# The stick-breaking scan takes the score tile in PSUM as its second operand, and the planner costs a scan at two cycles an element

## The chip, the cores and the metric

The kernel runs on one core of one Trainium2 chip. The metric is device time in microseconds (us), the median of several runs. The engines are named as in the profile: PE (TensorE matmuls), PEld (its weight loads), DVE (VectorE), ACT (ScalarE), POOL (GpSimd) and SP (the queue that issues the transfers). SBUF is the on-chip memory that all of them use, PSUM the small memory into which PE writes.

## The reference

A decoder trunk of two layers over one sequence of 1024 tokens, width 1024. Each layer is a mixing sub-layer (a stick-breaking attention branch and a latent-attention branch, fed by one input projection, gated and merged) and a squared-ReLU MLP of width 4096. The change touches only the weights of the stick-breaking branch: 8 heads of width 64, query blocks of 128 rows, each against all keys up to its own block.

```
z = q @ k.T * scale                                    # one block: 128 x end
log_fail = where(mask, log_sigmoid(-z), 0)
later    = reverse_cumsum(log_fail, keys) - log_fail
w        = where(mask, exp(log_sigmoid(z) + later), 0)
o        = w @ v
```

In products instead of logs: with F = sigmoid(-z) and W = sigmoid(z), the weight of key s is W[s] times the product of F over all later keys. Masked scores are so low that their F is 1 and their W is 0.

## The kernel before

**Recording and planning.** The program first records every operation (`record`) with its engine, its tiles and a duration from a table of costs (`cost`). A planner (`schedule`) then runs a list schedule with these durations: each of PE, ACT, DVE, POOL and the transfers picks, whenever it is free, the ready operation with the earliest due time. Due times are counted back from the order in which PE's operations were recorded. At last `emit` issues all operations by planned start time, and each engine works through its own queue strictly in that order. The semaphores between engines are put in by the framework beneath, from the order in which the operations are issued and the tiles that they touch. All helper calls go through line 213, so the profile's rows all read L213 and are told apart by tiles.

**One unit.** In the stick-breaking stage a layer works through 4 pairs of heads, 2 heads of a pair, 8 query blocks of a head: 64 units a layer, 128 in all. Block j has n = 128 (j + 1) keys. A unit is:

1. PE: scores into `sc`, a tile of 128 x 1024 in PSUM. There are two such tiles (`sc0`, `sc1`).
2. ACT: `F` = sigmoid(-z) and `W` = sigmoid(z), both read from `sc` and written to SBUF.
3. DVE: the scan, in place over `F`, from the last key to the first: a running product. Its second operation is `bypass`, so the second operand's values do not enter the result; before, that operand is `F` itself.
4. POOL: `W` times the scanned `F`, shifted by one key.
5. Two units later PE transposes `W` in groups of four blocks into `tp`, a PSUM tile of which there are two. ACT copies the group rounded to `wth`, DVE puts the rest into `wtl`; then the `tp` tile is free.
6. After every second unit PE multiplies `wth` and `wtl` with the values, into a `tp` tile again. ACT and DVE take the result out as `O`.

Between the units PE does "fill": the input projections of later pairs and gates (`pp<-H,parts`), whose weights are split by ACT and POOL (`parts`). In layer 0 the sums for the conditioning vector (`AD`, `A`) run on DVE as well. Then follows the latent-attention stage, the output projections and the MLP.

**The cost of a scan.** For DVE `cost` gives 0.069 us plus one cycle (1/960 us) an element, a scan included.

Of the kernel before, what the change touches and what calls it, by code (L numbers as in the profile page):

```python
# [15 lines left out]
ALU = mybir.AluOpType  # L16
# [159 lines left out]
class Plan:  # L176
# [13 lines left out]
    def record(self, engine, method, a, k):  # L190
# [14 lines left out]
        op.early = self.early  # L205
        op.func = str(k.get("func", "")).split(".")[-1]
        op.dur = cost(op.eng, method, a, k, outs, ins)
        op.succs, op.news, op.tiles = [], [], []
        nc = self.nc
# [216 lines left out]
def width(v):  # L426
    n = 1
    if v.dims is not None:
        for a, b in [(x, y) for _, x, y in v.dims[1:]]:
            n *= b - a  # L430
        return n
    for a, b in v.box[1:]:
        n *= b - a
    return n


def cost(eng, method, a, k, outs, ins):

    if eng == "DMA":
        v = (outs + ins)[0]  # L440
        n = 1
        for x, y in v.box:
            n *= y - x
        return n * 4 / 360e3
    n = width(outs[0])
    if eng == "PE":
        dt = str(ins[0].tile.dtype)
        if "32r" in dt:
            return 0.107 if n < 16 else (n if n >= 256 else 4 * n) / 2400.0 + 0.003
        if "bfloat" in dt:  # L450
            return n / 2400.0 + 0.003
        return 0.109 if method == "transpose" else 0.13
    psum = any(getattr(v.tile.cls, "psum", False) for v in ins)
    if eng == "ACT":
        x = 0.052 if psum else 0.093
        if isinstance(k.get("bias"), View):
            x += 0.093
        if k.get("accum_out") is not None:
            x += 0.093
        return x + n / 1200.0  # L460
    if eng == "DVE":
        if method == "reduce_max":
            n = width(ins[0])
        x = 0.069 + n / 960.0
        if method == "scalar_tensor_tensor" and len(ins) > 2:
            x += 0.06
        if method in ("tensor_scalar", "tensor_copy") and not psum:
            x = 0.069 + n / 1920.0 + (0.06 if len(ins) > 1 else 0)
        return x
    if method == "memset":  # L470
        return 0.036 + n / 1200.0
    if method == "tensor_scalar":
        return 0.26 + n * 3.33e-3
    return 0.15 + n * 2.1e-3
# [12 lines left out]
class Trunk:  # L487
# [553 lines left out]
    def sb_weights(self, ps, j):  # L1041
        nc = self.nc
        n = (j + 1) * P
        F, W = self.full(self.c_F), self.full(self.c_W)
        nc.scalar.activation(out=F[:, :n], in_=ps[:, :n], func=AF.Sigmoid, scale=-0.125)
        nc.scalar.activation(out=W[:, :n], in_=ps[:, :n], func=AF.Sigmoid, scale=0.125)
        rev = F[:, :n][:, ::-1]
        nc.vector.tensor_tensor_scan(out=rev, data0=rev, data1=rev, initial=1.0, op0=ALU.mult, op1=ALU.bypass)
        nc.gpsimd.tensor_mul(W[:, : n - 1], W[:, : n - 1], F[:, 1:n])
        return W  # L1050

# [658 lines left out]
```

## Time and profile before

| | us |
|---|---|
| Median of 3 runs | 3334.44 (3331.59 to 3336.16) |
| The profiled execution | 3345.88, its span 3344.1 |
| PE busy over the span | 3116.7 (93%) |
| DVE busy | 2295.3 (69%) |
| ACT busy | 1544.1 (46%) |
| POOL busy | 1243.2 (37%) |
| The 128 scans on DVE | 235.4 |

The two stick-breaking stages lie at about 294 to 606 us (layer 0) and 1990 to 2277 us (layer 1) of the span. A row of the timeline gives start, duration, engine, operation, output<-input, shape and, in brackets, how long the engine had stood idle and whose work ended that. In the rows by group the numbers behind the bar are busy time, mean duration in ns, and idle time of the engine just before.

### The profile page before, as it was taken

What the parts mean: (1) busy time and instruction counts of PE and PEld (TensorE: products, weight loads), DVE (VectorE), ACT (ScalarE), POOL (GpSimd) and SP (SyncE); (2) the same over time, 40 slices, a digit from 0 to 9 for tenths busy, and PEclk for the clock granted to TensorE, in tenths of its full rate; (3) what the DMA queues carried; (4) which work ended last, traced back from release to release, by engine and by line L of the source; (5) the groups of instructions that cost most, each with busy time, mean ns of one, the idle gap of its engine ahead of it and who ended that gap; (6) DMA issues with size and microseconds to landing.
All of it is one profiled execution on the core that took longest, in us unless ns stands there. A gap on an engine that the chain in (4) does not pass through costs nothing.

```text
span 3344.1 us, 42801 instructions
## 1 busy us (share of the span) xinstructions
PE 3116.7 (93%) x14823; PEld 2519.9 (75%) x14823; DVE 2295.3 (69%) x3238; ACT 1544.1 (46%) x2643; POOL 1243.2 (37%) x952
## 2 busy tenths in 40 slices
PE   5999899999998989998999998999999989999998
PEld 4877677778776777776777877778887767888886
DVE  7443677768567687799986326766675777658786
ACT  4443455657344434433344335556664444444434
POOL 3222344211234654344533223442112456544542
PEclk8999999999999999999999999999999999999999
DMA  6456455545844555876333474344457436467522
GB/s 216 148 164 187 119 150 141 143 129 155 273 128 126 187 189 174 258 237 206 104 103 91 131 219 130 105 126 108 112 167 243 133 104 204 155 199 255 181 76 89
DMA packets 450268, 532.46 MB, mean 159 GB/s; under 512 B 32498, under 2 KB 320900, under 8 KB 450052
## 3 DMA queue, kind: packets, MB, share of 16 engines
q1 hardware_dynamic: 450052, 529.72, 51.8%
q8 instruction: 118, 1.93, 0.3%
q14 instruction: 98, 0.80, 0.1%
HBM read 367.60 MB, written 162.00 MB: 158 GB/s over the span
## 4 chain that ended last, share of the span: by engine, by line
PE 61%; DVE 18%; DMA 11%; issue 4%; ACT 3%; POOL 1%; SPq 1%; DVEq 0%; ACTq 0%; POOLq 0%
PE pp L213 50%; PE tp L213 7%; PE sc L213 4%; DVE A L213 4%; DVE T L213 3%; DVE F L213 3%; DMA AD<-in_w_ada 3%; DMA T<-dram 2%; DVE x L213 2%; DMA dram<-T 1%; DVE wtl L213 1%; DVE bo L213 1%; DVE u L213 1%; POOL parts L213 1%; DMA vT<-dram 1%
## 5 line engine op out<-in xcount | busy, mean ns | idle before, releaser
L213 PE MATMUL pp<-H,parts 128*128 128x512 f32 x4032 | 1060.4, 407 | 13.5 <-ACT H L213 11.4
L213 PEld LDWEIGHTS pp<-H,parts 128*128 128x128 f32 x4032 | 742.3, 191 | 165.4 <-ACT H L213 13.1
L213 PE MATMUL pp<-bo,ws 128*128 128x512 f32 x2688 | 642.4, 400 | 28.0 <-POOL ws L213 15.7
L213 POOL TENSOR_TENSOR parts<-raw,parts 128x1024 fp32r<-128x1024 f32 (+2 forms) x168 | 370.1, 2204 | 758.0 <-ACT parts L213 699.2
L213 PEld LDWEIGHTS pp<-bo,ws 128*128 128x128 f32 x2688 | 506.7, 190 | 151.0 <-POOL ws L213 18.8
L213 POOL TENSOR_TENSOR ws<-wr,ws 128x1024 fp32r<-128x1024 f32 x112 | 295.7, 2647 | 367.2 <-ACT ws L213 335.3
L213 PE MATMUL pp<-t,pw 128*128 128x512 f32 x1344 | 322.0, 397 | 9.8 <-ACT u L213 9.5
L213 PEld LDWEIGHTS pp<-t,pw 128*128 128x128 f32 x1344 | 251.0, 189 | 70.4 <-ACT u L213 10.5
L213 DVE TENSOR_TENSOR_SCAN F<-F 128x128 f32<-128x128 f32 (+7 forms) x128 | 235.4, 1848 | 90.3 <-ACT F L213 90.2
L213 ACT CAST parts<-raw 128x1024 fp32r<-128x1024 f32 (+2 forms) x168 | 151.9, 904 | 265.1 <-PE pp L213 228.0
L213 PE MATMUL pp<-b,pw 128*128 128x512 f32 x1008 | 248.6, 404 | 14.4 <-DVE u L213 14.4
L213 ACT CAST wth<-tp 128x512 fp32r<-128x512 f32 (+3 forms) x384 | 180.8, 481 | 153.1 <-PE tp L213 147.9
L213 DVE TENSOR_TENSOR wtl<-tp,wth 128x512 fp32r<-128x512 f32 (+3 forms) x384 | 205.5, 548 | 64.8 <-ACT wth L213 62.9
L213 POOL TENSOR_TENSOR W<-W,F 128x127 f32<-128x127 f32 (+7 forms) x128 | 168.6, 1321 | 210.4 <-DVE F L213 117.5
L213 DVE SCALAR_TENSOR_TENSOR x<-pp,const,x 128x512 f32<-128x512 f32 x256 | 181.7, 740 | 90.6 <-PE pp L213 90.6
L213 POOL TENSOR_TENSOR pw<-T,pw 128x512 fp32r<-128x512 f32 x112 | 165.0, 1489 | 208.5 <-ACT pw L213 208.0
L213 PEld LDWEIGHTS pp<-b,pw 128*128 128x128 f32 x1008 | 191.3, 192 | 62.0 <-DVE u L213 17.4
L213 DVE SCALAR_TENSOR_TENSOR A<-AD,const,A 128x256 f32<-128x256 f32 x280 | 211.6, 756 | 30.7 <-DMA AD<-in_w_ada 27.2
L213 PE MATMUL tp<-const,W 128*128 128x128 f32 x1152 | 187.4, 277 | 44.3 <-DVE wtl L213 34.8
L213 ACT CAST bo<-T 128x512 fp32r<-128x512 f32 x224 | 135.4, 620 | 163.6 <-DMA T<-dram 106.1
L213 PEld LDWEIGHTS tp<-const,W 128*128 128x128 f32 x1152 | 138.4, 142 | 87.3 <-DVE wtl L213 26.0
L213 DVE TENSOR_TENSOR bo<-T,bo 128x512 fp32r<-128x512 f32 x224 | 192.1, 904 | 15.6 <-ACT bo L213 15.2
(151 smaller groups left out, 4614.5 us busy)
## 6 DMA issues: line engine op xcount, KB each, us to landing
T<-dram SPq DMA_DIRECT2D x352, 256.0 KB
dram<-T SPq DMA_DIRECT2D x208, 256.0 KB
dram<-u SPq DMA_DIRECT2D x92, 512.0 KB
AD<-in_w_ada SPq DMA_DIRECT2D x160, 256.0 KB
raw<-in_w_in SPq DMA_DIRECT2D x70, 512.0 KB
wr<-in_w_down SPq DMA_DIRECT2D x64, 512.0 KB
pr<-in_w_up SPq DMA_DIRECT2D x56, 512.0 KB
sq<-dram SPq DMA_DIRECT2D x96, 256.0 KB
```

Source lines behind the costliest of these rows:

```text
L213: getattr(getattr(nc, engine), method)(*[r(x) for x in a], **{n: r(x) for n, x in k.items()})
```

## The change

The scan's second operand becomes the same columns of the score tile `sc` in PSUM, and the planner's cost of a scan becomes 0.069 us plus two cycles an element.

```diff
@@ cost
         x = 0.069 + n / 960.0
+        if method == "tensor_tensor_scan":
+            x += n / 960.0
@@ sb_weights
         rev = F[:, :n][:, ::-1]
-        nc.vector.tensor_tensor_scan(out=rev, data0=rev, data1=rev, initial=1.0, op0=ALU.mult, op1=ALU.bypass)
+
+        over = ps[:, :n][:, ::-1]
+        nc.vector.tensor_tensor_scan(out=rev, data0=rev, data1=over, initial=1.0, op0=ALU.mult, op1=ALU.bypass)
         nc.gpsimd.tensor_mul(W[:, : n - 1], W[:, : n - 1], F[:, 1:n])
```

The built programs differ in order from the stick-breaking stage of a layer to somewhere in its latent-attention stage; the projections after it and the MLP have the same order as before. In the order the scan is printed as SCALAR_TENSOR_TENSOR, numbers behind names tell tiles apart, and the words in square brackets are the semaphores that an instruction waits for (DVE_49 means that something on DVE must be done).

First place, ACT's queue in layer 1, second pair, second head, from the block of 768 keys on (`F_18341` and `W_18357` are the unit of 768 keys, `F_18371` the next one). Before:

```order
L213 CAST parts_18329<-raw_17903 128x1024 [waits DMAHW0_49,PE_49]
L213 ACTIVATE F_18341<-sc_18331 128x768 [waits PE_49,Pool_49]
L213 CAST wth_18205<-tp_18337 128x4x128 [waits PE_49]
L213 ACTIVATE W_18357<-sc_18331 128x768
L213 CAST wth_18365<-tp_18354 128x4x128 [waits PE_49]
L213 ACTIVATE F_18371<-sc_18346 128x896 [waits Pool_49]
```

The same place of the changed kernel:

```order
L213 CAST parts_18329<-raw_17903 128x1024 [waits DMAHW0_49,PE_49]
L213 ACTIVATE F_18341<-sc_18331 128x768 [waits PE_49,Pool_49]
L213 CAST wth_18202<-tp_18337 128x4x128 [waits PE_49]
L213 ACTIVATE W_18357<-sc_18331 128x768 [waits DVE_49]
L213 CAST wth_18364<-tp_18354 128x4x128 [waits PE_49]
L213 ACTIVATE F_18369<-sc_18346 128x896 [waits Pool_49]
```

The order is the same, but `W` now waits for DVE: the scan of this unit reads the same PSUM tile and was issued before it. Of the 128 units, 67 have `W` issued after their scan and wait so (before, 2 of the 128 waited for DVE at all); in 43 `W` is issued between `F` and the scan, and in 18 before `F`, and there the scan waits for `W`.

Second place, DVE's queue in layer 1, third pair, first head, from the block of 768 keys on (`F_18741` is its scan, `F_18759` that of 896 keys, `F_18798` and `F_18806` that of 1024). Before:

```order
L213 SCALAR_TENSOR_TENSOR F_18741<-F_18741 128x768 [waits Activation_49]
L213 TENSOR_TENSOR wtl_18506<-tp_18739,wth_18491 128x4x128 [waits Activation_49]
L213 SCALAR_TENSOR_TENSOR F_18759<-F_18759 128x896 [waits Activation_49]
L213 TENSOR_TENSOR wtl_18783<-tp_18753,wth_18767 128x4x128 [waits Activation_49]
L213 TENSOR_TENSOR wtl_18552<-tp_18775,wth_18538 128x128 [waits Activation_49]
L213 SCALAR_TENSOR_TENSOR F_18798<-F_18798 128x1024 [waits Activation_49]
```

The same place of the changed kernel:

```order
L213 SCALAR_TENSOR_TENSOR F_18741<-F_18741,sc_18713 128x768 [waits Activation_49]
L213 TENSOR_TENSOR wtl_18503<-tp_18739,wth_18490 128x4x128 [waits Activation_49]
L213 TENSOR_TENSOR wtl_18780<-tp_18753,wth_18765 128x4x128 [waits Activation_49]
L213 SCALAR_TENSOR_TENSOR F_18759<-F_18759,sc_18733 128x896 [waits Activation_49,Pool_49]
L213 TENSOR_TENSOR wtl_18549<-tp_18785,wth_18533 128x128 [waits Activation_49]
L213 TENSOR_TENSOR T_18818<-pp_18655,T_18783 128x512 [waits DMAHW4_49]
L213 SCALAR_TENSOR_TENSOR F_18806<-F_18806,sc_18777 128x1024 [waits PE_49,Activation_49,Pool_49]
```

The second `wtl` of four blocks has moved from behind the scan of 896 keys to ahead of it. The second and the fourth pair of the layer show the same move.

## Rows read from the trace of the kernel before

**Rows 1.** Busy us (x) of PE, PEld, DVE, ACT, POOL by stage; clock, DMA share, GB/s.

```profile
294.00:606.00 312.00, 272.51 (x1487) 217.66 (x1485) 217.14 (x268) 157.27 (x302) 133.03 (x142) 0.97 0.52 142
1990.00:2277.00 287.00, 258.71 (x1435) 208.42 (x1434) 185.92 (x204) 153.43 (x293) 122.62 (x135) 0.98 0.47 126
```

**Rows 2.** Who waited for whom, 294 to 606 us: us in total, times, longest.

```profile
PE tp L213 <- DVE wtl L213: 25.4, 23, 5.1
...
PEld tp L213 <- POOL W L213: 8.3, 4, 5.6
PE tp L213 <- DVE O L213: 6.7, 6, 2.1
...
PE sc L213 <- ACT F L213: 1.4, 1, 1.4
```

**Rows 3.** The same view, 1990 to 2277 us.

```profile
PE tp L213 <- DVE wtl L213: 21.3, 22, 2.0
...
PE tp L213 <- DVE O L213: 1.8, 4, 0.6
```

**Rows 4.** Chain that ended last, shares by line, of 294:606 and of 1990:2277.

```profile
by line: PE pp L213 18.2%; DVE F L213 16.7%; PE tp L213 14.3%; issue 7.6%; DVE A L213 5.7%; DVE wtl L213 5.7%; DMA AD<-in_w_ada 5.0%; DMA sq<-dram 4.5%; PE sc L213 4.2%; DMA vT<-dram 3.5%; ACT F L213 2.3%; DMA dram<-lt 1.9%; DMA mq<-dram 1.
...
by line: PE pp L213 25.0%; PE tp L213 17.1%; DVE F L213 15.9%; DMA vT<-dram 5.7%; DVE wtl L213 5.7%; issue 5.7%; DMA dram<-T 4.7%; PE sc L213 4.2%; ACT F L213 3.9%; DMA sq<-dram 3.5%; DMA dram<-lt 2.5%; ACT W L213 1.7%; ACT parts L213 1.4%;
```

**Rows 5.** All scans as one group, and those of 768 keys alone.

```profile
L213 DVE TENSOR_TENSOR_SCAN F<-F 128x128 f32<-128x128 f32 (+7 forms) x128 | 235.4, 1848 | 90.3 <-ACT F L213 90.2
...
L213 DVE TENSOR_TENSOR_SCAN F<-F 128x768 f32<-128x768 f32 x16 | 40.2, 2511 | 27.9 <-ACT F L213 27.9
```

**Rows 6.** Timeline, third pair, first head, blocks of 768 and 896 keys.

```profile
2166.37 1.76 DVE L213 TENSOR_TENSOR_SCAN F<-F 128x768 f32<-128x768 f32 x1 [0.42 <-ACT F L213]
...
2168.27 1.54 POOL L213 TENSOR_TENSOR W<-W,F 128x767 f32<-128x767 f32 x1 [2.86 <-DVE F L213]
2168.62 3.06 DVE L213 TENSOR_TENSOR_SCAN F<-F 128x896 f32<-128x896 f32 x1
...
2171.61 0.85 DVE L213 TENSOR_TENSOR wtl<-tp,wth 128x512 fp32r<-128x512 f32 x2
...
2172.32 0.19 PEld L213 LDWEIGHTS tp<-wth,V 128*128 128x128 f32 x1 [1.78 <-DVE wtl L213]
```

**Rows 7.** Timeline, layer 1, second pair, second head, block of 768 keys.

```profile
2125.60 2.39 POOL L213 TENSOR_TENSOR parts<-raw,parts 128x1024 fp32r<-128x1024 f32 x1 [3.22 <-ACT parts L213]
...
2126.38 3.22 DVE L213 TENSOR_TENSOR_SCAN F<-F 128x768 f32<-128x768 f32 x1 [4.59 <-ACT F L213]
...
2129.63 1.29 DVE L213 TENSOR_TENSOR wtl<-tp,wth 128x512 fp32r<-128x512 f32 x2
...
2130.38 0.33 PE L213 MATMUL tp<-const,W 128*128 128x128 f32 x1 [1.99 <-DVE wtl L213]
```

**Rows 8.** Four tiles' DVE instructions: duration ns min/median/max, first and last start.

```profile
L213 DVE TENSOR_TENSOR_SCAN F<-F x128: 411/1750/4206, 304.7 to 2277.3; 128x128 f32<-128x128 f32 x16, 128x256 f32<-128x256 f32 x16, 128x384 f32<-128x384 f32 x16, 128x512 f32<-128x512 f32 x16
...
L213 DVE TENSOR_TENSOR bo<-T,bo x224: 668/679/2931, 1387.7 to 3293.0; 128x512 fp32r<-128x512 f32 x112
...
L213 DVE TENSOR_TENSOR wtl<-tp,wth x384: 256/608/693, 319.4 to 2500.4; 128x512 fp32r<-128x512 f32 x128, 128x128 fp32r<-128x128 f32 x32, 128x384 fp32r<-128x384 f32 x32
...
L213 DVE SCALAR_TENSOR_TENSOR x<-pp,const,x x256: 729/739/752, 934.2 to 3326.1; 128x512 f32<-128x512 f32 x128
```

**Rows 9.** Timeline of DVE, two scans beside which POOL did nothing.

```profile
2039.26 0.67 DVE L213 TENSOR_TENSOR_SCAN F<-F 128x256 f32<-128x256 f32 x1
...
2205.74 2.29 DVE L213 TENSOR_TENSOR_SCAN F<-F 128x1024 f32<-128x1024 f32 x1 [0.62 <-ACT F L213]
```

**Rows 10.** ACT's groups: the casts to `wth` and the sigmoids `W`.

```profile
L213 ACT CAST wth<-tp 128x512 fp32r<-128x512 f32 (+3 forms) x384 | 180.8, 481 | 153.1 <-PE tp L213 147.9 <-POOL wth L213 0.8
...
L213 ACT ACTIVATE W<-sc 128x128 f32<-128x128 f32 (+7 forms) x128 | 83.8, 666 | 15.9 <-DMA dram<-lt 10.9 <-PE sc L213 4.9
```

**Rows 11.** Waits over the whole span: DVE's scans for ACT's `F`.

```profile
DVE F L213 <- ACT F L213: 90.2, 51, 12.1
```

## The prediction

> **What bounds the kernel now.** First the busy times of the two stick-breaking stages, since nothing else is changed. PE is busy for 272.5 of 312 us in layer 0 and for 258.7 of 287 us in layer 1; DVE is next with 217.1 and 185.9 us, and ACT and POOL have room [rows 1]. So PE sets the pace and stands idle for 39.5 + 28.3 = 67.8 us in both stages together. That is the most that any change here can win, 2% of the run. The waits tell what ends the idle time: `wtl` on DVE for 25.4 us and `O` on DVE for 6.7 us in layer 0 [rows 2], 21.3 and 1.8 us in layer 1 [rows 3], 55.2 us in all. PE has its next transposes ready but both `tp` tiles are still being emptied by DVE. For POOL's products it waits for 8.3 us, for a score tile 1.4 us [rows 2]. The chain of waits says which DVE work is in front of those `wtl`: scans are 16.7% of the chain in layer 0 and 15.9% in layer 1 [rows 4], that is 0.167 x 312 + 0.159 x 287 = 52.1 + 45.6 = 97.7 us. Of 235.4 us of scans [rows 5], 41.5% lie on the chain.
>
> **What a scan costs now.** The scans of 768 keys take 2.51 us on average [rows 5], but one of them takes 1.76 us, with POOL idle until its end [rows 6], and one 3.22 us, for 1.61 us of which POOL splits a weight, reading SBUF [rows 7]: 1.46 us longer, nearly the whole overlap. DVE instructions with both tensors in SBUF show the same elsewhere: `bo` has a median of 679 ns and a longest of 2931 ns. Those with one input in PSUM and one in SBUF don't: `wtl` never exceeds 693 ns in 384, `x` stays within 729 to 752 ns in 256 [rows 8]. So the stretching belongs to the second SBUF input. That is what the change takes away; it doesn't depend on the value being used.
>
> **Term 1, shorter scans.** Undisturbed scans take 0.67 us for 256 keys and 2.29 us for 1024 [rows 9], a line of 0.13 us plus 2.11 ns an element. Over the eight widths (4608 elements) that is 8 x 0.13 + 4.608 x 2.11 = 10.8 us, for 16 of each 172 us in place of 235.4: 63 us of DVE. No row has a scan with a PSUM operand. If PSUM doesn't help, the gain is nothing; if every scan is undisturbed, 63 us. I take the second, because `wtl` and `x` are the nearest rows and show no price for PSUM. Of this 41.5% lies on the chain: **-26.2 us**. It is no more, because the rest of the scans hides under PE's fill today.
>
> **Term 2, the planner.** At twice the cycles the planned scan of 576 keys (the average) takes 1.27 us, near the 1.35 us of the line above, where it was 0.67. The order shows one clear effect. In the third pair's first head DVE took the scan of 896 keys (3.06 us) ahead of the second `wtl`, and PE's weight load stood for 1.78 us until that was done [rows 6]. Now that `wtl` comes first. A shorter scan alone would give back 3.06 - 2.02 = 1.04 us of it; the move gives the remaining 0.74 us, in three pairs of layer 1: **-2.2 us**. Other moves I can't price from rows and take at nothing; their bounds are in the rivals.
>
> **Term 3, scans that wait for W.** Both readers of the score tile now have an order. In 43 units the scan waits for `W`, of 0.666 us on average [rows 10], 28.6 us in all. Today 51 of the 128 scans find DVE idle and start as soon as `F` is there [rows 11]; for the other scans DVE is still busy and the wait is covered. 28.6 x 51/128 = 11.4 us of DVE standing, at the chain's share of 41.5%: **+4.7 us**. In the 18 units with `W` ahead of `F` nothing changes, since the scan needs `F` anyway.
>
> **Term 4, W that waits for the scan.** In 67 units `W` stands in ACT's queue until the scan is done, and everything behind it stands too. Where three or more ACT instructions lie between `F` and `W` (36 units) the scan is done by then, and I take nothing. In 31 units there are only one or two. By the order 8 of them have 128 keys, 8 have 768, 7 have 1024 and 8 lie between; their scans add up to 45 us on the line above; less 0.48 us for a cast to `wth` in each [rows 10], 15 us, ACT stands for 30 us. The example is the unit of [rows 7]: the scan starts at 2126.38 as soon as `F` is there, a cast follows `F` on ACT, and `W` stands from about 2126.9 to 2128.1 us. Behind it are the next cast to `wth` and the next `F`. A cast that comes late keeps a `tp` tile, for which PE waits; in 14 of the 31 units a cast is among the next two instructions, 30 x 14/31 = 13.6 us. The second `tp` tile covers part; I take **+10 us**, with bounds of nothing and 30. In this example the balance is still good: the scan ends at 2128.14 instead of 2129.60, and the first `wtl` behind it frees PE, which stood for 1.99 us until 2130.38. POOL's product starts later by `W`, but `W` is transposed only two units later and PE waits for products for 8.5 us at most, so I add nothing for it.
>
> **Term 5, the score tile.** It is held until scan and `W` are done, not only `F` and `W`. A unit comes every 599/128 = 4.7 us, and with two tiles each has 9.4 us. For the widest unit I allow 2 us for the scores, 2.29 for the scan and 0.666 x 1024/576 = 1.2 for each of `F` and `W`, 6.7 us. The cover is the other tile; I take **nothing**. If that cover is gone, all 110 units of terms 3 and 4 pass on their `W`: 110 x 0.666 = 73.3 us.
>
> **Sum.** -26.2 - 2.2 + 4.7 + 10 = -13.7 us. The profiled execution took 3345.9 us, 11.5 more than the median; it becomes 3332.2, and the median 3334.4 becomes 3320.7. I forecast **3321 us**, its own range 3310 to 3327.
>
> **Rivals.**
>
> *The serial order eats the gain (no change).* `W`, until now beside the scan, lies in series with it in 110 units. If all 73.3 us weigh as much as scans do, 41.5%, that is +30.4 in place of the +14.7 of terms 3 and 4: -28.4 + 30.4 = +2.0, 3336 us. For it speaks that every long `W` comes right before or after a long scan; against it that in the long units DVE was the busy one, so that DVE seldom stands when `W` runs. The Trainium skill, "PSUM — Partial Sum Buffer", section "PSUM bank collisions raise a hardware error", states that two engines may not read one bank and quadrant of PSUM at a time, so that ScalarE and VectorE reads have to be ordered by semaphores; by that the waits can't be had away, and the full +30.4 us would be their price. The order agrees on the waits; no run here shows a collision.
>
> *Score tiles run short (slower).* PE finds no free score tile because `W` behind the scan, or the scan behind `W`, releases it late, and the matmuls queued behind the scores in PE's strict order stand as well. The planner doesn't know of this order between readers and places scores too early. With a share s of the 73.3 us the run becomes 3320.7 + 73.3 s; at s = 0.28 it is slower by 0.2%. At s = 0.42, taken as typical, it is 3351 us. Against it: 1.4 us of such waits today, and 6.7 us of need in 9.4. For it: nothing in the planner keeps a distance between `F`, the scan and `W`, and units don't come evenly. A scan that doesn't get shorter would end in the same place (3334.4 + 14.7 = 3349); [rows 8] leave little room for that.
>
> *The planner's truer cost does more (much faster).* If the new order and the shorter scans remove two thirds of the 55.2 us that DVE makes PE wait and ACT's stalls are covered by the fill, the run is 3334.4 - 36.8 = 3298 us. For it: the moved `wtl`. Against it: the planner still knows nothing of `W` and scan in series.
>
> **Chances and range.** Forecast 0.38, much faster 0.13, no change 0.24, slower 0.25. What a measurement of this kernel can tell is about 0.2%, 6.7 us. The forecast's lower neighbours give faster by over 0.2% a chance of 0.5, within 0.2% 0.26, slower 0.24. The range 3300 to 3350 leaves out the far half of both outer cases.
>
> **What the profile would show.** Term 1: scans in one narrow duration for each width, 1.76 us at 768 keys and 2.29 at 1024, 172 us in all. Terms 3 and 4: ACT's `W` waiting for DVE `F`, about 30 us, and DVE `F` waiting for ACT's `W`. Result: PE's waits for `wtl` and `O` falling from 55 to about 40 us in the two stages, which get shorter by some 14 us in sum. Wrong, if PE waits for `sc` behind DVE `F` or ACT `W` by over 20 us (slower), or if scans are still stretched beside POOL, or if the stages after these change by more than a few us, since their order is the same except at the start of the latent attention.

## The result, and the profile after

The changed kernel takes 3287.89 us (median of 4 runs, 3285.35 to 3293.0), the kernel before 3333.02 us beside it: a ratio of 0.9871, 95% interval 0.9847 to 0.9894, or 45 us less. The forecast was 3321 us with a range from 3300. The direction was right; the gain is three times the forecast one and lies beyond the range.

The profiled execution took 3293.0 us, its span 3291.2. The stages lie at other times of the span now, so each window below is moved with its stage; its margins differ from those of [rows 1] by at most 2.2 us. Busy us (x) of PE, PEld, DVE, ACT and POOL by stage, then clock, DMA share and GB/s:

```profile
295.00:579.00 284.00, 265.74 (x1486) 214.01 (x1485) 189.91 (x267) 156.73 (x303) 124.22 (x142) 0.99 0.57 156
1957.00:2225.00 268.00, 255.70 (x1442) 207.63 (x1441) 153.00 (x203) 154.64 (x295) 115.31 (x134) 0.99 0.50 135
```

The stages are 552 us long in place of 599. PE stands idle for 18.3 + 12.3 = 30.6 us in them, where it was 67.8: 37.2 us less. The other 9.8 us are busy time: PE is busy for 521.4 us where it was 531.2, at a mean granted clock of 0.99 of 2.4 GHz after 0.97 and 0.98. The two profiled executions lie 52.9 us apart (3345.9 and 3293.0), the medians 45, so what is added up from this pair of traces may be a few us too large.

Who waited for whom in layer 0, the stretch 295 to 579 us (total us, times, longest):

```profile
ACT W L213 <- DVE F L213: 20.8, 15, 2.2
...
PE tp L213 <- DVE O L213: 6.2, 5, 2.2
...
DVE F L213 <- ACT W L213: 4.9, 5, 2.1
...
PE sc L213 <- DVE F L213: 4.2, 3, 2.7
PE tp L213 <- DVE wtl L213: 3.7, 10, 0.7
PE sc L213 <- ACT W L213: 3.0, 6, 0.9
```

The same view of layer 1, 1957 to 2225 us:

```profile
ACT W L213 <- DVE F L213: 12.6, 12, 2.0
...
DVE F L213 <- ACT W L213: 9.3, 11, 1.0
...
PE sc L213 <- ACT W L213: 2.5, 6, 0.5
...
PE tp L213 <- DVE wtl L213: 2.0, 4, 0.5
...
PE tp L213 <- DVE O L213: 0.7, 1, 0.7
...
PE sc L213 <- DVE F L213: 0.4, 2, 0.2
```

Two things are to be seen. PE's waits for `wtl` and `O` are 12.6 us, where [rows 2, 3] had 55.2. And there is a new kind: PE waits 10.1 us for a score tile that the scan or `W` still reads.

All scans as a group, and then those of 768 keys alone (busy us, mean ns, idle before), the answer to [rows 5]:

```profile
L213 DVE TENSOR_TENSOR_SCAN F<-F,sc 128x128 f32<-128x128 f32 (+7 forms) x128 | 171.7, 1349 | 99.1 <-ACT F L213 74.2
...
L213 DVE TENSOR_TENSOR_SCAN F<-F,sc 128x768 f32<-128x768 f32 x16 | 28.1, 1754 | 17.3 <-ACT F L213 14.9 <-POOL W L213 1.5 <-ACT W L213 0.9
```

And the unit of [rows 7], 768 keys in layer 1, second pair, second head, on the timeline (start, duration; in brackets the idle time before it and what ended it):

```profile
2082.99 2.40 POOL L213 TENSOR_TENSOR parts<-raw,parts 128x1024 fp32r<-128x1024 f32 x1 [0.21 <-ACT parts L213]
...
2083.77 1.75 DVE L213 TENSOR_TENSOR_SCAN F<-F,sc 128x768 f32<-128x768 f32 x1 [1.48 <-ACT F L213]
...
2085.56 0.81 ACT L213 ACTIVATE W<-sc 128x768 f32<-128x768 f32 x1 [1.34 <-DVE F L213]
...
2086.42 0.53 PEld L213 LDWEIGHTS sc<-sq,sq 128*128 128x128 f32 x3 [0.85 <-ACT W L213]
2086.43 0.96 PE L213 MATMUL sc<-sq,sq 128*128 128x512 f32 x3 [0.42 <-ACT W L213]
```

The scan takes 1.75 us instead of 3.22, although POOL splits a weight beside it for nearly all of that time, until 2085.39 us. `W` starts when the scan ends, ACT having stood for 1.34 us, and the next scores have to wait for `W`, PE for 0.42 us: the chain scan, `W`, score tile, PE that the forecast priced in terms 3 to 5.

### The profile page after: what moved, and what is told of

The parts are those of the page before. It is cut to its first block, busy times and chain, and to the rows that moved or that the text cites. A ratio compares the mean times of both kernels' runs of the same rounds, so it can differ in the third digit from the quotient of the medians.

```text
span 3291.2 us, 42785 instructions
## 1 busy us (share of the span) xinstructions
PE 3103.3 (94%) x14823; PEld 2510.8 (76%) x14823; DVE 2258.7 (69%) x3238; ACT 1544.9 (47%) x2643; POOL 1229.2 (37%) x952
## 5 line engine op out<-in xcount | busy, mean ns | idle before, releaser
L213 PE MATMUL pp<-H,parts 128*128 128x512 f32 x4032 | 1060.2, 407 | 10.5 <-ACT H L213 8.9
L213 PE MATMUL pp<-t,pw 128*128 128x512 f32 x1344 | 323.4, 398 | 10.7 <-ACT u L213 10.0
L213 DVE SCALAR_TENSOR_TENSOR A<-AD,const,A 128x256 f32<-128x256 f32 x280 | 223.3, 797 | 26.6 <-DMA AD<-in_w_ada 23.2
L213 DVE TENSOR_TENSOR_SCAN F<-F,sc 128x128 f32<-128x128 f32 (+7 forms) x128 | 171.7, 1349 | 99.1 <-ACT F L213 74.2
L213 POOL TENSOR_TENSOR W<-W,F 128x127 f32<-128x127 f32 (+7 forms) x128 | 155.2, 1217 | 209.7 <-ACT W L213 122.8
L213 DVE TENSOR_TENSOR bo<-T,bo 128x512 fp32r<-128x512 f32 x224 | 201.4, 946 | 18.3 <-ACT bo L213 17.9
L213 ACT ACTIVATE u<-u 128x1024 f32<-128x1024 f32 x112 | 118.7, 1060 | 149.1 <-DVE u L213 142.6
```

What stands on the lines that cost most here:

```text
L213: getattr(getattr(nc, engine), method)(*[r(x) for x in a], **{n: r(x) for n, x in k.items()})
```

## Experiments

Each run was timed in five rounds against the kernel before on the same chip. All times are medians, this kernel's first and then the kernel before; brackets hold the 95% interval of the ratio. "Own operand" means that the scan names `F` twice, as before.

### Which half of the change brings it

**The new order alone.** All engines have exactly the order of the changed kernel; when a scan is issued, its second operand is set back to `F`.

```diff
+            if method == "tensor_tensor_scan":
+                k["data1"] = k["data0"]
```

> Every instruction stands where it stands in the changed kernel (same order on all five engines), but the scan is issued with F itself as its second operand, as before; so scans are again stretched beside POOL (about 235 us in all) and ACT's W waits for no scan. Theory A (the shorter scan is what wins): the gain falls back to 0 to 12 us below before, 3321 to 3333 us, and PE's waits for wtl stay near 40 us. Theory B (the planner's truer cost wins: it puts wtl ahead of scans and spreads the units): 30 us or more of the 45 us stay, 3300 us or less. Theory C (each needs the other): under half of the gain, 3311 to 3325 us.

Measured: 3305.72 against 3332.57 us, 0.9918 [0.99, 0.9936], 27 us less. The waits that the order shortens (284 us of layer 0, 304 to 588 us, then 1982 to 2258 us of layer 1):

```profile
PE tp L215 <- DVE wtl L215: 9.2, 13, 1.5
...
PE tp L215 <- DVE O L215: 8.8, 6, 2.9
```

```profile
PE tp L215 <- DVE wtl L215: 7.9, 8, 1.4
...
PE tp L215 <- DVE O L215: 2.4, 3, 1.4
```

Waits for `wtl` and `O` are down to 28.3 us from 55.2, though the scans still take 227.3 us. The time falls between theories B and C: 27 us of the 45 stay, more than C's half and less than B's 30.

**The operand alone.** All engines keep the order of the kernel before; only when a scan is issued does it take the score tile as its second operand. The planner knows nothing of it. Shown are the lines that matter; `live` is true where the tile still holds the scores of this unit, and in the trace all 128 scans read it.

```diff
+        nc.over = ps[:, :n][:, ::-1]
@@ when the scan is issued
+                if live:
+                    k["data1"] = over
```

> Every instruction stands where it stood before (same order on all engines), but each scan reads the score tile as its second operand, with the waits between scan and W that this brings. Theory A: scans take 172 us in all as in the changed kernel and 30 us or more of the gain are there, 3303 us or less. Theory B: 3318 to 3333 us, PE's waits for wtl still above 30 us. Theory C: 3311 to 3325 us. If the waits between scan and W are dear, the time is near or above that of before, with PE waiting for sc.

Measured: 3324.08 against 3332.57 us, 0.9971 [0.9959, 0.9983], 8.5 us less. Waits in layer 0 (303 to 599.5 us):

```profile
ACT W L222 <- DVE F L222: 21.7, 18, 2.8
...
PE tp L222 <- DVE wtl L222: 13.3, 16, 1.6
...
PE sc L222 <- ACT W L222: 9.6, 7, 2.5
...
PE tp L222 <- DVE O L222: 4.2, 5, 2.1
PE sc L222 <- DVE F L222: 4.1, 4, 2.0
```

and in layer 1 (1978 to 2267 us):

```profile
ACT W L222 <- DVE F L222: 34.5, 30, 2.6
...
PE sc L222 <- ACT W L222: 11.3, 9, 1.5
...
PE sc L222 <- DVE F L222: 6.4, 6, 1.9
...
PE tp L222 <- DVE O L222: 4.7, 5, 1.2
...
PE tp L222 <- DVE wtl L222: 2.5, 5, 0.6
```

The scans take 171.2 us, and the waits for `wtl` and `O` fall to 24.7 us, 30.5 less than before. But PE now waits 31.4 us for score tiles (1.4 before). So the operand gives about 30 us and takes about 30 back; PE's idle time in the two windows is 61.6 us in all, 6.2 less than the 67.8 of before. (These waits come from one pair of profiled executions, 3345.9 and 3313.9 us, which lie further apart than the medians.) The time fits theories B and C, but B's other sign, waits for `wtl` above 30 us, did not come: they are 15.8.

**The planner's cost alone.** Two cycles an element in the plan, own operand.

```diff
+        if method == "tensor_tensor_scan":
+            x += n / 960.0
```

> The planner's half of the change alone: the scan at two cycles an element, F still its second operand. The order is nearly that of the changed kernel, so by the run with that exact order (3306 us) this lies at 3298 to 3314 us. If the operand's entry in the plan (the scan holding the score tile there) mattered, it is more than 10 us off that.

Measured: 3303.92 against 3335.93 us, 0.99 [0.9883, 0.9917], 32 us less. It agrees with the order alone: that order comes nearly whole from this one line (in 72 of DVE's 3238 places another instruction stands).

The halves don't add up: 8.5 + 27 = 35 us apart, 45 us together.

### What the planner's cost does

**Three cycles, own operand.**

```diff
+        if method == "tensor_tensor_scan":
+            x += 2 * n / 960.0
```

> Before, with F as second operand, but a scan costed at three cycles an element, 1.87 us for 576 keys, which is what the stretched scan takes on average (1.85 us). Theory B: a plan with the true cost of the slow scan wins 25 us or more, 3308 us or less. Theory A: less than 12 us, 3321 us or more, since DVE is as busy as before and the wtl behind stretched scans stay late.

Measured: 3283.75 against 3332.57 us, 0.985 [0.9828, 0.9872], 49 us less, as much as the whole change with its PSUM operand. For the average scan of 576 keys the plan's cost is now 0.069 + 3 x 576/960 = 1.87 us; before, the chip took 235.4/128 = 1.84 us for it and the plan 0.67.

**A busy engine or a late result?** A longer scan in the plan does two things: DVE is taken, so that other work is put in its place, and the scanned `F` comes later, so that POOL's product and the transposes come later. First the engine busy for three cycles, but the result there after one (due times still count three; `op.scan` marks a scan):

```diff
+                    if op.scan:
+                        end = now + (dur - 0.069) / 3 + 0.069
@@ cost
+        if method == "tensor_tensor_scan":
+            x += 2 * n / 960.0
```

> Before, with DVE busy for three cycles an element in the plan, but the scan's result there after one cycle, as before the change. Theory F: little, 3318 us or more. Theory G: most of the gain of three cycles, 3300 us or less. If both this and the one with late weights give about half, the two work together.

Measured: 3284.37 against 3335.93 us, 0.9841 [0.9822, 0.986], 51.6 us less. The page's row of its scans, and the `wtl` and `O` waits of layer 0 (302.5 to 574.5 us):

```profile
L214 DVE TENSOR_TENSOR_SCAN F<-F 128x512 f32<-128x512 f32 (+7 forms) x128 | 233.3, 1830 | 68.9 <-ACT F L214 68.6
```

```profile
PE tp L214 <- DVE wtl L214: 6.7, 4, 2.5
...
PE tp L214 <- DVE O L214: 2.6, 4, 1.2
```

Layer 1 adds 1.4 us for `wtl`. So the scans are as long as before (235.4 us), and still 55.2 us of waits have become 10.7. Then the other half: the scan stays at one cycle, and POOL's product is planned longer by two cycles an element, so that only what follows the scan is late.

```diff
+    if method == "tensor_mul":
+        return 0.15 + n * 2.1e-3 + 2 * n / 960.0
```

> Before, with the scan at one cycle, but the planner's cost of POOL's product raised by two cycles an element: the weights of a unit are as late in the plan as with a scan of three cycles (3284 us), while DVE looks as free as before. Theory F (the plan helps because transposes and later units are placed later): most of that gain, 3300 us or less. Theory G (the plan helps because DVE is taken for busy, so that wtl and O are put ahead of scans): little, 3318 us or more.

Measured: 3318.42 against 3335.93 us, 0.9939 [0.9922, 0.9957], 17.5 us less. So lateness, with the earlier due time that it gives the scan, brings a third of the gain by itself (POOL is planned busy for longer here as well, which this run doesn't separate), and a DVE that is held busy, with that due time too, brings all of it. The two overlap, since 17.5 and 51.6 us are more than the 49 of both together.

What the plan does with it can be added up from the traces. In the time from the end of a group's `wth` on ACT to the start of its `wtl`, over all 192 such groups of the two stages, DVE ran scans for 154.8 us before the change, for 141.5 us with the late product and for 91.9 us with the busy scan (119.6 us with the new order alone). The busy DVE of the plan puts `wtl` ahead of scans, as theory G has it.

### What the planner doesn't know: scan and W in series

**The scan told to follow W.** The changed kernel, with the scan recorded as depending on `W`, so that the plan has `W` read the tile first and the scan after it.

```diff
+        nc.ops[-1].preds.add(nc.ops[-2].i)
```

> The changed kernel, with the planner told that a scan comes after W of its unit, so that no W waits for a scan any more and each of the 128 scans waits for its W. If the waits that the planner didn't know of cost what terms 3 and 4 of the prediction say (about 15 us), this is 5 to 15 us faster than the changed kernel, 3273 to 3283 us. If they are covered, it is within 5 us of it, 3283 to 3293 us; if starting each scan later by W lies on the path, it is slower, above 3295 us.

Measured: 3259.54 against 3332.57 us, 0.9783 [0.9763, 0.9803], 73 us less, 28 us below the changed kernel. That is more than any of the three expected outcomes, and about twice what terms 3 and 4 say. ACT's `W` no longer waits for a scan at all, and PE's waits for score tiles are down to one of 1.7 us (layer 0, 303 to 571.4 us):

```profile
PE tp L213 <- DVE wtl L213: 9.2, 7, 4.2
...
PE sc L213 <- DVE F L213: 1.7, 1, 1.7
...
PE tp L213 <- DVE O L213: 1.6, 1, 1.6
```

In layer 1 PE waits neither for `wtl`, nor for `O`, nor for score tiles. Busy us by stage, layer 0 and then layer 1:

```profile
303.00:571.40 268.40, 255.19 (x1461) 210.67 (x1460) 185.61 (x268) 156.34 (x302) 121.02 (x141) 0.99 0.58 158
1955.00:2210.70 255.70, 252.15 (x1474) 211.34 (x1473) 157.62 (x212) 157.85 (x300) 116.52 (x140) 0.99 0.50 139
```

So PE's idle time is 16.8 us, 13.8 less than in the changed kernel; 8.4 us of the difference are waits for score tiles. PE's busy time is 507.3 us, where the changed kernel has 519.4 between the same points (304 to 583 and 1967 to 2238 us). Why the busy time falls too, no run here shows.

**The other direction.** `W` is recorded behind the scan and depends on it.

```diff
-        nc.scalar.activation(out=W[:, :n], in_=ps[:, :n], func=AF.Sigmoid, scale=0.125)
@@ behind the scan
+        nc.scalar.activation(out=W[:, :n], in_=ps[:, :n], func=AF.Sigmoid, scale=0.125)
+        nc.ops[-1].preds.add(nc.ops[-2].i)
```

> The changed kernel at two cycles, with the planner told the other order: W of a unit after its scan, so that all 128 W wait for their scan on ACT and no scan waits for W. If it is the planner's knowledge that counts, whichever way round, within 10 us of 3260 us. If a W that holds up ACT's queue is what costs (term 4 of the prediction), it is slower than that, 3270 us or more, since W comes after the scan in every unit.

Measured: 3263.94 against 3333.53 us, 0.9796 [0.9775, 0.9817]. Nearly the same: that the plan knows the order matters more than which one it is. `W` still stands 23.6 us for scans here (13.1 and 10.5 us by layer), but no wait of PE's matmuls for a score tile is left.

### Both together

**The changed kernel at three cycles** (its cost line is `x += 2 * n / 960.0`).

> The changed kernel with the scan costed at three cycles in place of two; its scans take 1.35 us on average, so this cost is too high by half. If what helps is that the planned cost is true, this is no better than the changed kernel, 3285 us or more. If it helps because a longer planned scan also leaves room for the waits of W that the planner doesn't know of, it is 10 to 25 us faster, 3263 to 3278 us.

Measured: 3270.39 against 3333.53 us, 0.9808 [0.979, 0.9826], 17.5 us below the changed kernel, although a scan with its operand in PSUM takes 1.35 us on average and three cycles are 1.87.

**W first, at three cycles** (that cost line and the dependence).

> The told PSUM version (each scan after its W, 3260 us) with three cycles in place of two. If the planned cost is best when true, it is 0 to 10 us slower, 3260 to 3270 us; if a longer planned scan is always better, it is faster than 3255 us.

Measured: 3250.07 against 3333.53 us, 0.9747 [0.973, 0.9765], the fastest of all and 38 us below the changed kernel. Busy us by stage, 303.1 to 561.0 and 1940.8 to 2196.0 us:

```profile
303.10:561.00 257.90, 250.53 (x1448) 209.11 (x1446) 188.61 (x264) 154.02 (x298) 118.99 (x140) 0.99 0.57 160
```

```profile
1940.80:2196.00 255.20, 248.29 (x1428) 207.56 (x1427) 154.06 (x205) 153.53 (x293) 114.29 (x134) 0.99 0.49 136
```

PE stands idle for 7.4 + 6.9 = 14.3 us in both: little idle time is left.

**W first, at four cycles** (`x += 3 * n / 960.0`).

> The told PSUM version at four cycles an element, nearly twice what the scan takes. Two cycles gave 3260 us, three 3250 us. If room in the plan always helps, below 3250 us; if the planned cost has an optimum near what unit and waits take together, 3253 us or more, since DVE looks full to the planner and fill runs out before the units do.

Measured: 3265.4 against 3335.93 us, 0.9786 [0.9767, 0.9804]. Two, three and four cycles give 3259.5, 3250.1 and 3265.4 us. Three is the best of these; its interval is clear of that of four cycles and just touches that of two.

**The same cost and order of W and scan, with its own operand.** Three cycles and `W` first, but the scan names `F` twice. The plan is not quite the same: a scan that doesn't read the score tile doesn't hold it in the plan either, and in 362 of DVE's 3238 places another instruction stands.

> The scan reads F itself again, as before the change, with the planner at three cycles an element and told that a scan comes after W of its unit. Scans are stretched beside POOL (about 225 us in all) and nothing on the chip orders scan and W. Theory D (only the plan counts; a plan that fits the scan that runs is as good with either operand): within 10 us of the 3260 us of the told PSUM version, 3250 to 3270 us. Theory E (the shorter scan is worth something of its own once the plan fits): 3275 us or more.

Measured: 3254.66 against 3333.53 us, 0.9763 [0.9746, 0.978]. Its scans take 205.1 us, and the interval overlaps that of the version with PSUM, 0.973 to 0.9765. So a good plan with its own operand comes within 4.6 us, by the medians, of the one with the PSUM operand, on which the forecast built nearly all its gain; that is not told from nothing. What the operand alone is worth in one and the same good order was not measured.

## Why the prediction was wrong

**The step that failed is term 2, the planner.** It priced one kind of move at -2.2 us, and "Other moves I can't price from rows and take at nothing". The order alone gives -27 us and the cost alone -32. The argument saw a planned scan of 0.67 us beside one of 1.84 on the chip, and asked only which rows had visibly moved. It didn't ask what the gap does: in the old plan DVE is free after about a third of the time that the chip needs, so that due work behind a scan seems to be in time, and on the chip `wtl` stands behind scans for 154.8 us. With DVE held busy in the plan, and scans on the chip as long as before, the waits for `wtl` and `O` fall from 55.2 to 10.7 us (the run with the result after one cycle), and that standing to 91.9. In the changed kernel these waits fall to 12.6 us, where the forecast looked for about 40, and the stages get 47 us shorter in place of 14. This is the rival "The planner's truer cost does more", whose 3298 us and chance of 0.13 were both too cautious. That the cost's truth explains all of it is not shown: for a PSUM scan two cycles are nearly right, and three are better by 17.5 us. Why, stays open.

**Term 1, shorter scans: right in duration, near in worth.** Forecast 172 us in all, 1.76 at 768 keys and 2.29 at 1024; measured 171.7, 1.754 and 2.283. With the order held, the waits for `wtl` and `O` fall by 30.5 us, forecast 26.2. The Trainium skill, "SBUF — State Buffer", section "Who interferes with whom", says that a VectorE instruction with two SBUF inputs contends with GpSimd's reads, and that one with at most one SBUF input doesn't, outside the modes that use both port pairs; the scans agree, 2.51 us before and 1.75 after at 768 keys.

**Terms 3 and 4, the new waits: right in length, not in their path.** Scans stand 14.2 us for `W` (forecast 11.4), `W` stands 33.4 us for scans (forecast 30). They came from the order and the durations of before. But the waits by engine put no wait of PE down to a late cast to `wth`, the way by which term 4 got its +10 us; what PE pays shows at the score tile, which term 5 had at nothing. What these waits cost in time was not measured by itself.

**Term 5, the score tile at nothing: wrong, most of all in the old order.** In the old order with the new operand PE waits 31.4 us for score tiles. That is the rival "Score tiles run short", with s = 31.4/73.3 = 0.43, near the 0.42 that it took as typical. Its cost and the gain of term 1 cancel, so terms 1, 3, 4 and 5 together (-11.5 us) come near the operand alone (-8.5) partly by luck. The new plan spends longer on a scan and, since the scan now reads the score tile, holds the tile until it is done; there these waits are 10.1 us, and with the order of `W` and scan told 1.7. The rival's own sentence, that the planner doesn't know of this order and places scores too early, is borne out in part: telling it brings 28 us, of which 8.4 are waits for score tiles.

**The rivals "no change" and "slower".** The serial order of the two readers is real and costs ACT 33.4 us, but PE only 10.1. The Trainium skill, "PSUM — Partial Sum Buffer", section "PSUM bank collisions raise a hardware error", states that accesses of two engines to the same bank and partition quadrant must be kept apart by semaphores; the waits agree, and no run here shows a collision. What was taken for a fixed price is mostly one of placing: with `W` planned first ACT doesn't wait for scans, and with the scan planned first it does, for 23.6 us, at nearly the same time of the run.

**Of PE's busy time the forecast said nothing, and so its bound was too low.** It called PE's 67.8 us of idle time the most that any change here can win. Five of the runs win more, up to 83 us. With `W` first, idle time gives 51 us (67.8 to 16.8) and busy time 23 (530.2 us before, from 303 to 610 and from 2001 to 2292 us, to 507.3). In the changed kernel the busy time is 9.8 us less for the stages at a granted clock of 0.99 after 0.97 and 0.98. Over the whole span the clock is 0.980 or 0.981 in the four runs of the changed kernel, and 0.974 to 0.979 in the 37 runs of the kernel before that were timed beside the experiments, so these ranges lie apart and the clock seems to go with the kernel. But the own operand at three cycles is 49 us faster as well and has 0.976 to 0.978, so less standing alone doesn't bring it. What lowers PE's busy time stays open.

## What to carry to other kernels

Where a planner orders the work, compare its costs with the durations in the trace first, engine by engine: a cost that is too low by a factor on a busy engine can be worth more than making the instruction itself shorter, and it is one line to try. When a new operand makes two engines read one PSUM tile, tell the planner of the order that the framework will put in, in either direction. And hold the order fixed when an operand is to be judged, for here the operand's gain and its new wait were about 30 us each and showed as 8.5.

## What the runs showed that was not expected

The stretching went both ways, at some widths. POOL's products of 383 elements in layer 1 took 1640 ns before and 864 after, as the rows by form show, first before (1990 to 2277 us), then after (1957 to 2225 us):

```profile
L213 POOL TENSOR_TENSOR W<-W,F 128x383 f32<-128x383 f32 x8 | 13.1, 1640 | 9.0 <-DVE F L213 9.0
```

```profile
L213 POOL TENSOR_TENSOR W<-W,F 128x383 f32<-128x383 f32 x8 | 6.9, 864 | 15.4 <-DVE F L213 8.3 <-ACT W L213 7.0
```

With the order held the operand alone does it: in the order of before these products take 869 ns over both layers with the operand alone (1199 in layer 0 and 1640 in layer 1 without it), and in the new order 1318 ns with the own operand, 864 in the changed kernel. In layer 1 the products of 127 elements shortened too (529 to 411 ns), those of the six other widths stayed within 1%.

And a scan costs the same with its second operand in PSUM as an undisturbed one with both in SBUF: 2.283 us on average at 1024 keys, 2.29 in [rows 9].
